# Row-wise largest absolute value: two-row loads into a column ring, a computed tail, and loads through GpSimd's queue

## The chip, the cores and the metric

The kernel runs on one core of a Trainium2 chip. The metric is the device time of one execution in microseconds. The time of before is the median of 10 runs.

## The reference

The input is a matrix of 8192 x 8192 float32 (268.4 MB). For each row the largest absolute value is wanted, 8192 numbers:

```python
def reference(x):
    return np.linalg.norm(x, ord=np.inf, axis=1)
```

## The kernel before

The rows are cut into 64 blocks of 128. In a block each row lies on its own partition, and its 8192 columns lie along the partition. For each block t the kernel takes one of five rotating buffers `xt` (128 x 8192, 32 KB a partition), loads the block by SP's queue (`nc.sync.dma_start`, L55) and reduces it on VectorE (L59: `tensor_reduce` with max and absolute value). The result is one column of `res`, which is 128 x 64.

The first 54 blocks are loaded in one piece of 4 MB. The last ten follow the list `COOLDOWN`: seven blocks in two pieces of 4096 columns, one in 4096, 2048, 2048, one in four of 2048, one in 2048, 2048, 1536, 1280, 1280. A block in pieces leaves its maxima in `partial`, and a second reduction (L68) joins them into `res`. That makes 80 loads in all.

After the loop `make_identity` builds a unit matrix on GpSimd (its work is done in the first 1.3 us of the trace, since nothing stands before it there). TensorE transposes `res` into PSUM (L78), VectorE copies it to SBUF (L80), and one store of 64 rows of 128 numbers ends the kernel (L81).

The framework puts in all waits: a load into `xt` waits until the reduction of the block five back has read that buffer, and a reduction waits for its load. It also sets the order of each engine's queue: it keeps the order of the program among what is ready, and takes what is ready sooner ahead of what still waits.

Of the kernel before, what the change touches and what calls it, by code (L numbers as in the profile page):

```python
# [1 line left out]

# [5 lines left out]


COOLDOWN = (
    [[4096, 4096]] * 7
    + [[4096, 2048, 2048]]
    + [[2048, 2048, 2048, 2048]]
    + [[2048, 2048, 1536, 1280, 1280]]
)


@with_exitstack
def kernel(  # L20
    ctx: ExitStack,
    tc: tile.TileContext,
    x: bass.AP,
    out: bass.AP,
):
    nc = tc.nc
    P = 128
    n_rows, n_cols = x.shape
    assert n_rows % P == 0

    T = n_rows // P
    if n_cols == 8192 and T >= len(COOLDOWN):
        chunks = [[n_cols]] * (T - len(COOLDOWN)) + COOLDOWN
    else:
        chunks = [[n_cols]] * T

    x_t = x.rearrange("(t p) m -> t p m", p=P)

    pool = ctx.enter_context(tc.tile_pool(name="sbuf", bufs=5))
    single = ctx.enter_context(tc.tile_pool(name="single", bufs=1))  # L40
    psum_pool = ctx.enter_context(tc.tile_pool(name="psum", bufs=1, space=bass.MemoryType.PSUM))

    res = single.tile([P, T], mybir.dt.float32)
    maxch = max(len(c) for c in chunks)
    if maxch > 1:
        partial = single.tile([P, maxch], mybir.dt.float32)

    for t in range(T):
        ch = chunks[t]
        assert sum(ch) == n_cols  # L50
        xt = pool.tile([P, n_cols], x.dtype)
        off = 0
        for h, w in enumerate(ch):
            dst = res[:, t : t + 1] if len(ch) == 1 else partial[:, h : h + 1]
            nc.sync.dma_start(  # L55
                out=xt[:, off : off + w],
                in_=x_t[t, :, off : off + w],
            )
            nc.vector.tensor_reduce(  # L59
                out=dst,  # L60
                in_=xt[:, off : off + w],
                axis=mybir.AxisListType.X,
                op=mybir.AluOpType.max,
                apply_absolute_value=True,
            )
            off += w
        if len(ch) > 1:
            nc.vector.tensor_reduce(  # L68
                out=res[:, t : t + 1],
                in_=partial[:, : len(ch)],  # L70
                axis=mybir.AxisListType.X,
                op=mybir.AluOpType.max,
            )

    ident = single.tile([P, P], mybir.dt.float32)
    make_identity(nc, ident)
    res_t_psum = psum_pool.tile([T, P], mybir.dt.float32)
    nc.tensor.transpose(res_t_psum, res, ident)  # L78
    res_t = single.tile([T, P], mybir.dt.float32)
    nc.vector.tensor_copy(out=res_t, in_=res_t_psum)  # L80
    nc.sync.dma_start(out=out.rearrange("(t p) -> t p", p=P), in_=res_t)  # L81


# [1 line left out]
_INS = ['x']  # L85
_OUTS = [((8192,), 'float32')]


# [23 lines left out]
```

## Time and profile before

| what | us |
|---|---|
| median of 10 runs | 634.68 (634.54 to 634.91) |
| profiled execution, its own time | 634.92 |
| its span in the profile | 633.1 |
| VectorE busy | 559.0 (91 instructions) |
| POOL (GpSimd) busy | 0.7 (6 instructions) |
| loads issued | 80, all by SP's queue |
| a 4 MB load, issue to landing, median | 39.8 |
| the store, issue to landing | 1.8 |

The span runs from the first instruction of the program to the last thing that the profile records; the execution's own time has some 1.8 us around it. "SPq" is SP's queue, which only issues transfers here. Idle time of an engine is given with what ended it ("<-DMA xt<-in_x_dram" is a load into `xt`). DMA slices are fortieths of the span, 15.83 us each.

### The profile page before, as it was taken

To read this page: it belongs to the slowest core of one execution; us is meant where nothing else is said; L and a number is where in the kernel's file an instruction comes from. 1 tells how busy PE (TensorE), PEld (TensorE's weight loads), DVE (VectorE), ACT (ScalarE), POOL (GpSimd) and SP (SyncE) were. 2 spreads that over 40 slices of the span, in tenths; PEclk is the share of its full clock that TensorE was granted. 3 is DMA by queue.
4 is the path that set the end of the run, shared out by engine and by line. 5 is a ranking of instruction groups with operands and counts; after the bars stand their busy time and mean duration, and the time that the engine had idled before them with its cause. 6 is when DMAs were issued, how large, how long until landed. Compare 5 with 4: busy or idle time off the path is not lost.

```text
span 633.1 us, 294 instructions
## 1 busy us (share of the span) xinstructions
PE 0.4 (0%) x1; PEld 0.1 (0%) x1; DVE 559.0 (88%) x91; POOL 0.7 (0%) x6
## 2 busy tenths in 40 slices
PE   0000000000000000000000000000000000000000
PEld 0000000000000000000000000000000000000000
DVE  1988988988989889889898898898988989999997
POOL 0000000000000000000000000000000000000000
DMA  9999999999999999999999999999999999999995
GB/s 373 435 439 435 435 431 433 433 431 431 431 431 431 431 431 431 431 431 431 431 431 435 433 429 431 431 435 435 437 433 437 431 431 417 426 430 424 428 422 212
DMA packets 11602, 268.49 MB, mean 424 GB/s; under 512 B 1296, under 2 KB 1360, under 8 KB 1744
## 3 DMA queue, kind: packets, MB, share of 16 engines
q1 hardware_dynamic: 11600, 268.47, 98.9%
q14 instruction: 2, 0.02, 0.0%
HBM read 268.44 MB, written 0.03 MB: 424 GB/s over the span
## 4 chain that ended last, share of the span: by engine, by line
DMA 75%; DVE 24%; SPq 0%; issue 0%; PE 0%; DVEq 0%
DMA xt<-in_x_dram 75%; DVE res L59 15%; DVE partial L59 8%; SPq L55 0%; DVE res L68 0%; PE res_t_psum L78 0%; DVE res_t L80 0%; DVEq L59 0%
## 5 line engine op out<-in xcount | busy, mean ns | idle before, releaser
L59 DVE TENSOR_REDUCE res<-xt 128x1 f32<-128x8192 f32 x54 | 469.0, 8686 | 67.6 <-DMA xt<-in_x_dram 67.6
L59 DVE TENSOR_REDUCE partial<-xt 128x1 f32<-128x4096 f32 (+3 forms) x26 | 88.2, 3430 | 3.0 <-DMA xt<-in_x_dram 2.8
L68 DVE TENSOR_REDUCE res<-partial 128x1 f32<-128x2 f32 (+3 forms) x10 | 1.6, 156 | 0.3
L80 DVE COPY res_t<-res_t_psum 64x128 f32<-64x128 f32 x1 | 0.3, 282 | 0.6 <-PE res_t_psum L78 0.6
L78 PE MATMUL res_t_psum<-ident,res 128*64 128x128 f32 x1 | 0.4, 393 | 629.7 <-DVE res L68 629.7
masks.py:199 POOL TENSOR_SCALAR_AFFINE_SELECT ident<-ident 128x128 f32<-128x128 f32 x1 | 0.3, 292 | 0.1
L78 PEld LDWEIGHTS res_t_psum<-ident,res 128*64 128x64 f32 x1 | 0.1, 128 | 629.7 <-issue 629.7
masks.py:197 POOL MEMSET ident<- 128x128 f32 x1 | 0.2, 204 | 0.3 <-POOLq L96 0.3
L96 POOL MEMSET const-bfloat16-1.0<- 128x1 bf16 x1 | 0.1, 102 | 0.0
L96 POOL MEMSET const-uint8-127<- 128x1 uint8 x1 | 0.1, 102 | 0.0
L96 POOL MEMSET const-float32-0.0<- 128x1 f32 x1 | 0.1, 98 | 0.2 <-issue 0.2
L96 POOL MEMSET const-float32-1.0<- 128x1 f32 x1 | 0.1, 98 | 0.0
## 6 DMA issues: line engine op xcount, KB each, us to landing
xt<-in_x_dram SPq DMA_DIRECT2D x54, 4096.0 KB, 39.8
xt<-in_x_dram SPq DMA_DIRECT2D x15, 2048.0 KB, 39.0
xt<-in_x_dram SPq DMA_DIRECT2D x8, 1024.0 KB, 28.3
xt<-in_x_dram SPq DMA_DIRECT2D x2, 640.0 KB, 17.9
xt<-in_x_dram SPq DMA_DIRECT2D x1, 768.0 KB, 19.3
out_dram<-res_t SPq DMA_DIRECT2D x1, 32.0 KB, 1.8
```

Of the source, the lines that this page charges most:

```text
L59: nc.vector.tensor_reduce(out=dst, in_=xt[:, off : off + w], axis=mybir.AxisListType.X, op=mybir.AluOpType.max, apply_absolute_value=True,)
L68: nc.vector.tensor_reduce(out=res[:, t : t + 1], in_=partial[:, : len(ch)], axis=mybir.AxisListType.X, op=mybir.AluOpType.max,)
L78: nc.tensor.transpose(res_t_psum, res, ident)
L80: nc.vector.tensor_copy(out=res_t, in_=res_t_psum)
L96: nc = _bacc.Bacc("TRN2", target_bir_lowering=False, num_devices=1)
```

## The change

The diff replaces the five buffers by one ring of 3 x 16384 columns (192 KB a partition) with 16 columns of padding behind it, and works as follows.

- **Large loads.** Two neighbouring rows go to one partition, so that a load takes 128 runs of 64 KB, 8 MB in all. One reduction makes both maxima (`res_big[:, t, :]`). There are `n_big` such loads, and the ring holds three.
- **Tail.** `tail_pieces` works the last blocks out backwards from a last piece of 1088 columns. It has a cost for a load and one for a reduction (`LOAD`, `REDUCE`: us a column, us each), and makes each earlier piece as large as the time lets it. With these constants it gives 14 blocks of 128 rows in 28 pieces: seven of 8192 columns, four of 4096 + 4096, then 2432, 2432, 3328, then 1728, 1728, 2496, 2240, and last 1408, 1472, 1600, 1408, 1216, 1088. So `n_big` is 25, and there are 53 loads.
- **Waits written by hand.** Each load counts on one of eight semaphores of the kernel's own, and its reduction waits on that. A load also waits for the reduction eight loads back. Where a load overwrites what a reduction reads, the framework still puts in the wait.
- **Joining.** The maxima of a tail block in pieces are joined by `tensor_scalar` with max on GpSimd (nine in all), in the place of L68. The last block's partial maxima are put into the columns just behind its last piece, so that its last reduction takes them along.
- **Output.** TensorE transposes the maxima of the large blocks and of the tail blocks but the last, ScalarE copies them, and SP stores them (two stores, `store_early`). The last block's 128 maxima are transposed in 32 x 32 squares on VectorE and stored as four lines of 32.
- **Queue.** All loads are issued by GpSimd (`self.nc.gpsimd.dma_start`), which makes their descriptors in software, in the place of SP's hardware queue. `make_identity` stands ahead of them in the program, on the same engine.

The diff, cut to its core:

```diff
+R = 2
+RING = 3 * 16384
+PAD = 16
+SEMS = 8
+LOAD = (1.1775e-3, 0.075)
+REDUCE = (1.0417e-3, 0.060)
+FIRST = 1088
+GRAIN = 64
+
+def tail_pieces(n_cols, big):
+    slack = 0.0
+    lag = REDUCE[0] * FIRST + REDUCE[1]
+    rows = []
+    while True:
+        left, row = n_cols, []
+        while left:
+            w = FIRST if not rows and not row else int((lag + slack - REDUCE[1]) / REDUCE[0])
+            w = max(GRAIN, w // GRAIN * GRAIN)
+            if w >= left:
+                w = left
+            elif 2 * w > left:
+                w = (left // 2 + GRAIN - 1) // GRAIN * GRAIN
+            row.append(w)
+            left -= w
+            slack += (LOAD[0] - REDUCE[0]) * w + LOAD[1] - REDUCE[1]
+        rows.append(row[::-1])
+        if (lag + slack - REDUCE[1]) / REDUCE[0] > big:
+            return rows[::-1]
...
+    def load(self, at, w, src):
+        i = self.started
+        self.started += 1
+        ins = self.nc.gpsimd.dma_start(out=self.ring[:, at : at + w], in_=src)
+        ins.then_inc(self.sems[i % SEMS], 16)
...
+        if i >= SEMS:
...
+            self.tc.add_manual_dep(
+                ins.ins,
+                self.reductions[i - SEMS].name,
...
+    def reduce(self, dst, src):
+        i = len(self.reductions)
+        ins = self.nc.vector.tensor_reduce(
...
+        ins.wait_op(self.sems[i % SEMS], 16 * (i // SEMS + 1), "sem-ge")
...
-    for t in range(T):
-        ch = chunks[t]
...
-            nc.sync.dma_start(
-                out=xt[:, off : off + w],
-                in_=x_t[t, :, off : off + w],
-            )
...
+    make_identity(nc, ident)
+    pieces = Pieces(tc, ring)
+
+    for t in range(n_big):
+        at = pieces.room(R * n_cols)
+        pieces.load(at, R * n_cols, x_big[t])
+        buf = ring[:, at : at + R * n_cols]
+        pieces.reduce(res_big[:, t, :], buf.rearrange("p (r m) -> p r m", r=R))
...
+    for t, widths in enumerate(tail):
...
+        for w, at in zip(widths, spots):
+            pieces.load(at, w, x_tail[t, :, col : col + w])
+            col += w
+        for i, (w, at) in enumerate(zip(widths, spots)):
+            behind = n - 1 if final and i == n - 1 else 0
+            pieces.reduce(parts[i], ring[:, at : at + w + behind])
+        if n > 1 and not final:
+            best = parts[0]
+            for i in range(1, n):
+                dst = res_tail[:, t : t + 1] if i == n - 1 else parts_t[:, n + i - 1 : n + i]
+                nc.gpsimd.tensor_scalar(
+                    out=dst, in0=best, scalar1=parts[i], scalar2=None, op0=mybir.AluOpType.max
+                )
+                best = dst
+    store_early()
+
+    turn = nc.vector.transpose(out=last_t, in_=last)
+    pieces.after_loads(turn)
+    tc.declare_fence(turn.ins, group="loads")
+    nc.sync.dma_start(
+        out=out_tail[n_tail - 1].rearrange("(b k) -> b k", k=32),
+        in_=last_t.rearrange("(b c) k -> c b k", c=32)[0],
+    )
```

## Prediction

> **What bounds the kernel now.** I read the page first: engine shares, then the two rows of slices, then the costliest groups.
>
> ```profile
> span 633.1 us, 294 instructions
> PE 0.4 (0%) x1; PEld 0.1 (0%) x1; DVE 559.0 (88%) x91; POOL 0.7 (0%) x6
> DMA  9999999999999999999999999999999999999995
> GB/s 373 435 439 435 435 431 433 433 431 431 431 431 431 431 431 431 431 431 431 431 431 435 433 429 431 431 435 435 437 433 437 431 431 417 426 430 424 428 422 212
> L59 DVE TENSOR_REDUCE res<-xt 128x1 f32<-128x8192 f32 x54 | 469.0, 8686 | 67.6 <-DMA xt<-in_x_dram 67.6
> ```
>
> VectorE is 88% busy, but its idle time ends on a load: 67.6 us before the 54 big reductions. The DMA engines are full in every slice but the last; only the first (373 GB/s), the tail (417 to 430) and the last (212) stand below 431. So the loads set the time, and three places are left: the start, what a load costs beside its bytes, and what follows the last landing. The timeline gives all three.
>
> ```profile
> 12.96 8.69 DVE L59 TENSOR_REDUCE res<-xt 128x1 f32<-128x8192 f32 x1 [12.96 <-DMA xt<-in_x_dram]
> 22.67 8.69 DVE L59 TENSOR_REDUCE res<-xt 128x1 f32<-128x8192 f32 x1 [1.02 <-DMA xt<-in_x_dram]
> ...
> 527.93 8.69 DVE L59 TENSOR_REDUCE res<-xt 128x1 f32<-128x8192 f32 x1 [1.02 <-DMA xt<-in_x_dram]
> ...
> 577.82 4.42 DVE L59 TENSOR_REDUCE partial<-xt 128x1 f32<-128x4096 f32 x1 [0.40 <-DMA xt<-in_x_dram]
> ...
> 587.61 4.42 DVE L59 TENSOR_REDUCE partial<-xt 128x1 f32<-128x4096 f32 x1 [0.41 <-DMA xt<-in_x_dram]
> ```
>
> Each reduction here starts when its load lands. 53 steps from 12.96 to 527.93 give 9.716 us for a 4 MB row block in one load. A block in two loads takes 587.61 - 577.82 = 9.79. The second load costs 0.074 us, and the bytes (9.716 - 0.074) / 8192 = 1.177 ns a column. The first landing, 12.96, less one step leaves 3.24 us that are spent once: some 2.15 before data flow at full rate (the first slice moved 5.90 MB in 15.83 us, at the later 431.7 GB/s 13.68 us of work), some 1.1 from a load's last bytes to the reduction. All 524,288 columns in 80 loads: 617.1 + 5.9 = 623.0; plus 3.24, the last landing is at 626.2. The end is then
>
> ```profile
> 620.49 8.92 DVE L59 TENSOR_REDUCE partial<-xt 128x1 f32<-128x2048 f32 x5
> 629.44 0.16 DVE L68 TENSOR_REDUCE res<-partial 128x1 f32<-128x5 f32 x1
> 629.75 0.39 PE L78 MATMUL res_t_psum<-ident,res 128*64 128x128 f32 x1 [629.75 <-DVE res L68]
> 630.18 0.28 DVE L80 COPY res_t<-res_t_psum 64x128 f32<-64x128 f32 x1 [0.58 <-PE res_t_psum L78]
> 630.49 0.55 SPq L81 DMA_DIRECT2D out_dram<-res_t  x1
> ```
>
> VectorE is about 3.2 us behind when the data are in; then a combining reduction, TensorE, a copy, and 2.6 us of store. That is 6.9 us after the last landing.
>
> **What the Trainium skill says.** "DMA: Bandwidth & Descriptors" (Latency and other measured facts) puts the first byte of a software-generated load at about 1 us, of a hardware one at 0.6; before has only the second kind. The same page (Issuing engines are not separate DMA queues) says that all issuers end on the same 16 engines; no run here shows loads from GpSimd. Its Bandwidth section fits software loads as 2.0 us plus bytes / 436e3, nearly the 435 GB/s that 1.177 ns a column means, but lists 425 GB/s as the best it measured: I use these as the two ends. "SBUF — State Buffer" (Who interferes with whom) says that a reduction on VectorE never takes the ports it shares with GpSimd, so descriptor writing is not held up by it. Nothing before tests that, as POOL is done at 1.3 us.
>
> **The change, part by part.** The sizes that the diff works out are 25 loads of 16384 columns (8 MB), then 14 tail blocks of 28 pieces (the title says 31): seven of 8192, four of 4096+4096, then 2432, 2432, 3328; 1728, 1728, 2496, 2240; 1408, 1472, 1600, 1408, 1216, 1088.
>
> Fewer loads: 53 instead of 80 at 0.074 is -2.0 us, if a 64 KB run moves as fast per byte as a 32 KB one. Not shown before; I take the same, within 0.2% (1.2 us) either way.
>
> Start: POOL's queue has the constants and the identity first, and these end at 1.01 + 0.29 = 1.30 us, while SP issued its first load at 0.74. That is +0.56, and the skill's first-byte difference adds 0.4: +0.96. From below +0.56; from above I allow +4, as POOL may prepare its queue.
>
> Steady stretch: load i waits for the reduction three back, since the ring holds three. A big reduction takes 16384 x 1.042 ns + 0.15 = 17.2 us (slope and constant from the 8192 and 4096 rows, 8686 and 4417 ns), a load 19.36, so load i is issued some 21 us before its turn. One or two microseconds of descriptor making are hidden by that: zero. If the cover went, each of some 50 loads would show them.
>
> Tail: the wait for the reduction eight back leaves 11 us or more in the queue even at the last load, worked out from the same steps. Zero. On VectorE, a back-to-back reduction costs its columns x 1.042 ns + 0.063 (two of 4096 in 8.75 us). Stepping through the 28 pieces it starts 7.4 us behind after the last 8 MB piece, falls to 0.2 at the last piece, and never idles long enough to matter. The ten combining reductions of L68 (1.6 us) leave VectorE. In their place nine tiny maxima come to POOL's queue, between loads; each waits for a tail block's last reduction, and what is queued behind it is a later load. POOL's 128x1 memset takes 0.1 us; I take 0.2 for each maximum. The scheduler places what is ready sooner ahead, so I expect in front of a maximum only loads whose own wait ends earlier: zero; the other order is a rival.
>
> Early stores: three TensorE transposes, three ScalarE copies, two SP stores, all before the last block is in; 32 KB beside 268 MB is under 0.1 us, hidden by some 10 us of final-block loads.
>
> End: final reduction 1093 x 1.042 + 0.148 = 1.29; backlog 0.2; gaps 0.05; VectorE transpose of 32 columns 0.18 (the 5-column reduction takes 0.16; between 0.15 and 0.4); store and finish 2.61 as now. Sum 4.3 instead of 6.9.
>
> **Sum.** Last landing 3.24 + 0.96 + 617.1 + 3.9 = 625.2; plus 4.3 the span is 629.5 against 633.1: 2.0 from loads, 2.6 from the end, less 0.96. The profiled execution took 634.92, 1.8 more than its span, and the median is 634.68, 0.24 less. So 631.3 profiled, 631.1 as median; I put 0.4 on top for POOL's part of the start: 631.5.
>
> **Rivals.** Software loads are slower each or per byte. At 425 GB/s a column is 1.205 ns: +14.4 us, 645.5. At 0.2 us a load instead of 0.074, 53 x 0.126 = 6.7: 637.8. It decides from small numbers: 4.5 us spends the gain and 0.2% more, that is 0.085 us a load or 0.73% of rate. For it: the skill's 425, and that hardware generation already runs within 0.1% of the fit's ceiling, so a change can only lose. Against: each engine gets eight long runs for 19 us, little to generate or fetch. This is the main case on the slower side.
>
> The maxima block the loads. If POOL keeps the written order, after each of six tail blocks the next block's loads stand behind a maximum that waits for the block's last reduction. The DMA engines then run dry for 1.1 (landing) + 4.4 (reduction) + 0.1 + 0.2 (maximum) + about 2 (new load) = 7.8 us, thrice; 11.7 at the first, where VectorE is behind, 7.2 and 6.3 at the two with shorter pieces: 48.6 us in all, some 680.
>
> A costly start: POOL needs 3 to 6 us before its first load. All of it lies on the path: 633.5 to 637.
>
> The late start and the new end cancel, and loads gain nothing (64 KB runs slower by 0.3%): 633.5, no change.
>
> **How the numbers follow.** A difference of 0.2% (1.3 us) is about what a measurement of this kernel can tell from no change. My forecast, between 630 and 633.4, gets 0.48; no change (633.4 to 635.9), from a start of 2 to 4 us more or a rate 0.4% lower, 0.12; slower loads 0.25; a start beyond 5 us 0.05; blocked loads or a much worse rate 0.10. That is 0.48 faster, 0.12 same, 0.40 slower. The range runs from 629.3 (64 KB runs 0.2% quicker, start +0.56) to 646 (425 GB/s), leaving out the blocked case and what is worse. Since both signs count, the likeliest case's own range is 629.3 to 633.4.
>
> **What would show it.** Right: the first big reduction near 23.6 us (19.36 + 4.2), later ones 19.36 apart, slices at 431 to 435 GB/s from the second on, the queue's kind software, the last reduction 1.3 us long and ending near 626.7, 2.8 us before the end. Steps above 19.5 would show the slower loads; gaps in the slices after 560 us with POOL's maxima ahead of loads, the blocked queue; a first landing beyond 26 us, the start. A step of 19.45 or more, or a drained slice in the tail, makes the forecast wrong.

## The result, and the profile after

The changed kernel takes 645.19 us (median of 8 runs, 644.82 to 646.81), the kernel before 634.68. The ratio is 1.0167 with a 95% interval of 1.0158 to 1.0176: slower by 1.7%, where 631.5 us was forecast. The profiled execution took 645.17 us with a span of 643.0.

The page of the changed kernel, its span, engine shares and DMA slices (now 16.1 us each), its queue, and the big reductions:

```profile
span 643.0 us, 182 instructions
PE 1.0 (0%) x3; PEld 0.3 (0%) x3; DVE 552.9 (86%) x54; ACT 2.0 (0%) x4; POOL 31.3 (5%) x68
DMA  9999999999999999999999999999999999997896
GB/s 391 391 457 400 448 457 391 457 432 416 457 432 416 457 408 440 457 391 457 457 391 457 457 391 457 436 412 457 420 428 424 425 435 444 413 388 328 322 384 223
...
q0 software_dynamic: 7632, 268.44, 97.6%
...
L88 DVE TENSOR_REDUCE res_big<-ring 128x2 f32<-128x16384 f32 x25 | 430.5, 17220 | 75.4 <-DMA ring<-in_x_dram 75.4
```

For 34 of the 40 slices the loads run as before. The single slices are uneven now (391, 457), but their mean from the second on is 432 GB/s, as before. The loss is in the last slices: 413, 388, 328, 322, 384, where before had 417 to 430. The timeline of VectorE bounds it:

```profile
23.42 17.22 DVE L88 TENSOR_REDUCE res_big<-ring 128x2 f32<-128x16384 f32 x1 [23.42 <-DMA ring<-in_x_dram]
...
488.70 17.22 DVE L88 TENSOR_REDUCE res_big<-ring 128x2 f32<-128x16384 f32 x1 [2.14 <-DMA ring<-in_x_dram]
```

The first large load lands at 23.42 us (23.6 was forecast). The last lands at 488.70, which is (488.70 - 23.42) / 24 = 19.39 us a step, where 19.36 was forecast. Up to here the forecast is half a microsecond off. The rest is lost in the tail. There POOL's own timeline shows what its queue did (start, duration, instruction, idle time before it and what ended that):

```profile
532.00 1.05 POOL L72 DMA_DIRECT2D ring<-in_x_dram  x2 [7.55 <-DVE res_tail L88]
574.84 0.28 POOL L188 TENSOR_SCALAR res_tail<-parts 128x1 f32<-128x1 f32 x1 [41.79 <-DVE parts L88]
575.07 0.58 POOL L72 DMA_DIRECT2D ring<-in_x_dram  x1
583.49 0.27 POOL L188 TENSOR_SCALAR res_tail<-parts 128x1 f32<-128x1 f32 x1 [7.85 <-DVE parts L88]
583.72 1.10 POOL L72 DMA_DIRECT2D ring<-in_x_dram  x2
```

POOL issues a pair of loads at 532.00 ("x2") and then nothing for 41.79 us. It stands at the first joining maximum, which waits for a reduction on VectorE (`parts`). The next load comes the moment that the maximum is done, at 575.07, and the next again only behind the second maximum. The chain of work that ended last has the same steps (start, duration, what):

```profile
583.49 0.23 POOL res_tail L188
583.72 7.43 DMA ring<-in_x_dram
591.15 0.02 issue
591.17 4.43 DVE parts L88
595.60 0.09 issue
595.70 0.23 POOL res_tail L188
595.92 7.48 DMA ring<-in_x_dram
```

A maximum releases a load, the load lands 7.4 us later (4.8 us of bytes, the rest start and landing), the reduction takes 4.4 us, and only that releases the next maximum. So in the tail, loads and reductions take turns where they should run beside each other. The size follows from the rate at which the DMA engines moved data (the last number of each line, in GB/s). The first line is the changed kernel from 575 to 630 us. The second is the variant with all maxima last (below) in the same part of its tail, 575 to 620 us:

```profile
575.00:630.00 55.00, 0.39 (x1) 0.10 (x1) 45.01 (x14) 0.24 (x1) 9.82 (x23) 1.00 0.85 332
```

```profile
575.00:620.00 45.00, 0.39 (x1) 0.10 (x1) 45.00 (x15) 0.26 (x1) 8.20 (x21) 1.00 1.00 422
```

At 332 instead of 422 GB/s, 55 x (1 - 332 / 422) = 11.7 us are lost. VectorE's idle times in the tail, from the timeline, add up to 3.46 + 0.46 + 2.96 + 1.78 + 1.06 + 0.21 + 0.80 + 1.20 = 11.9 us. The two spans differ by 13.4 us. The rest of that: the tail begins 0.5 us later (505.84 against 505.32 us), and VectorE is busy 0.9 us longer (552.9 against 552.0).

### The profile page after: what moved, and what is told of

It is laid out like the page before. It is cut to its first block, busy times and chain, and to the rows that moved or that the text cites. A ratio compares the mean times of both kernels' runs of the same rounds, so it can differ in the third digit from the quotient of the medians.

```text
span 643.0 us, 182 instructions
## 1 busy us (share of the span) xinstructions
PE 1.0 (0%) x3; PEld 0.3 (0%) x3; DVE 552.9 (86%) x54; ACT 2.0 (0%) x4; POOL 31.3 (5%) x68
## 4 chain that ended last, share of the span: by engine, by line
DMA 59%; DVE 39%; issue 1%; POOL 0%; POOLq 0%; DVEq 0%
DMA ring<-in_x_dram 59%; DVE res_big L88 24%; DVE res_tail L88 9%; DVE parts L88 5%; DVE ring L88 1%; POOL res_tail L188 0%; DVE last_t L194 0%; POOL ident masks.py:197 0%; POOLq L188 0%; POOLq masks.py:199 0%; DVEq L88 0%; POOLq L213 0%
## 5 line engine op out<-in xcount | busy, mean ns | idle before, releaser
L88 DVE TENSOR_REDUCE res_big<-ring 128x2 f32<-128x16384 f32 x25 | 430.5, 17220 | 75.4 <-DMA ring<-in_x_dram 75.4
L88 DVE TENSOR_REDUCE parts<-ring 128x1 f32<-128x4096 f32 (+5 forms) x15 | 52.8, 3560 | 10.0 <-DMA ring<-in_x_dram 9.9
L88 DVE TENSOR_REDUCE res_tail<-ring 128x1 f32<-128x8192 f32 x7 | 60.2, 8675 | 0.0
L72 POOL DMA_DIRECT2D ring<-in_x_dram x53 | 28.5, 539 | 513.1 <-DVE res_big L88 489.2
L88 DVE TENSOR_REDUCE ring<-ring 128x1 f32<-128x1408 f32 (+4 forms) x6 | 9.3, 1573 | 2.1 <-DMA ring<-in_x_dram 2.0
L188 POOL TENSOR_SCALAR res_tail<-parts 128x1 f32<-128x1 f32 x6 | 1.6, 274 | 76.2 <-DVE parts L88 76.2
```

What stands on the lines that cost most here:

```text
L72: ins = self.nc.gpsimd.dma_start(out=self.ring[:, at : at + w], in_=src)
L88: ins = self.nc.vector.tensor_reduce(out=dst, in_=src, axis=mybir.AxisListType.X, op=mybir.AluOpType.max, apply_absolute_value=True,)
L188: nc.gpsimd.tensor_scalar(out=dst, in0=best, scalar1=parts[i], scalar2=None, op0=mybir.AluOpType.max)
```

## The experiments

**The maxima on VectorE.** The loads stay on GpSimd's queue.

```diff
-                nc.gpsimd.tensor_scalar(
+                nc.vector.tensor_scalar(
```

> The nine maxima go from GpSimd's queue to VectorE; all 53 loads stay on GpSimd's software queue. Blocked-queue theory: the eight idle stretches of VectorE in the tail of the changed kernel (3.46 + 0.46 + 2.96 + 1.78 + 1.06 + 0.21 + 0.80 + 1.20 = 11.9 us) go away, and nine maxima at about 0.16 us come to VectorE, whose backlog takes most of them: 631.8 to 634 us. Rival, software loads of a megabyte or less are slow in themselves: the idle stretches stay, since no load is changed, and the time is 643 to 647 us.

Measured: 633.68 us (633.38 to 633.92), 0.9983 of before (0.9976 to 0.9991). The idle stretches are gone: the waits table shows none of VectorE on loads in the tail. So loads of a megabyte or less are not slow in themselves. But VectorE is now busy without a break until the end, and each maximum takes 0.21 us there. The span (median 631.9) is 2.0 us longer than the next variant's (629.85), about nine times 0.21. The time is only 1.6 us longer, for a reason that the last section gives.

**The maxima behind the last load.** They stay on GpSimd, and only their place in the queue changes.

```diff
+            joins.append((t, n, parts, parts_t))
...
+    for t, n, parts, parts_t in joins:
...
+            ins = nc.gpsimd.tensor_scalar(
...
+            tc.add_manual_dep(
+                ins.ins,
+                pieces.last_load.name,
+                mybir.DependencyInfo(mybir.DependencyClass.NoSync, mybir.DependencyReason.DATA),
...
```

> The nine maxima stay on GpSimd, but all stand behind the last load in its queue. Blocked-queue theory: the loads are again limited only by the reduction eight back, VectorE does not wait in the tail, 631.5 to 633.5 us. Rival, that GpSimd computing at all slows its descriptor making or VectorE: the work is the same, so 640 us or more. Rival, slow small software loads: 643 to 647 us.

Measured: 632.05 us (631.82 to 632.29), 0.9957 of before (0.9942 to 0.9972), span 629.6. The instructions are the same (54 on VectorE, 68 on POOL, as in the changed kernel); the order in POOL's queue alone is worth 645.19 - 632.05 = 13.1 us. POOL's timeline of this variant, in the time in which the changed kernel's stood still:

```profile
531.48 1.05 POOL L72 DMA_DIRECT2D ring<-in_x_dram  x2 [7.54 <-DVE res_tail L89]
540.07 0.53 POOL L72 DMA_DIRECT2D ring<-in_x_dram  x1 [7.55 <-DVE res_tail L89]
548.67 0.53 POOL L72 DMA_DIRECT2D ring<-in_x_dram  x1 [8.07 <-DVE res_tail L89]
557.26 0.53 POOL L72 DMA_DIRECT2D ring<-in_x_dram  x1 [8.06 <-DVE res_tail L89]
565.85 0.53 POOL L72 DMA_DIRECT2D ring<-in_x_dram  x1 [8.06 <-DVE res_tail L89]
570.18 0.53 POOL L72 DMA_DIRECT2D ring<-in_x_dram  x1 [3.80 <-DVE parts L89]
```

Five loads were free to go between 540 and 570 us: their own waits ended there. In the changed kernel all five stood behind the first maximum.

**All loads on SP's hardware queue.**

```diff
-        ins = self.nc.gpsimd.dma_start(out=self.ring[:, at : at + w], in_=src)
+        ins = self.nc.sync.dma_start(out=self.ring[:, at : at + w], in_=src)
```

> The same kernel with its 53 loads on SP's hardware queue; the maxima stay on GpSimd. Every theory expects no blocked loads here. The prediction's sum without the 0.96 us of the later start is 630.1 to 630.6 us. If the software queue costs more than its start and its order, this is lower than the run with late maxima by more than 1.5 us; if the start is all, by 0.7 to 1.3 us.

Measured: 630.86 us (630.75 to 631.03), 0.9938 of before (0.9923 to 0.9953), span 628.6. This is the fastest of all versions, ahead of both kernels. The first landing is at 22.66 us instead of 23.81 with the maxima last, 1.15 earlier, and the whole is 1.2 us faster.

**The kernel before, with only its 80 loads on GpSimd's queue.**

```diff
-            nc.sync.dma_start(
+            nc.gpsimd.dma_start(
                 out=xt[:, off : off + w],
```

> The kernel before with only its 80 loads moved to GpSimd's queue; no other work stands between them there. Blocked-queue theory: only a later start, by 0.3 to 1 us, so 635 to 636 us. Rival, each software load costs some 0.2 us instead of 0.074: 80 x 0.126 = 10 us more, 645 us; rival, the rate is 425 GB/s: 649 us.

Measured: 635.55 us (635.31 to 635.94), 1.0014 of before (1.0007 to 1.0021), which is 0.9 us. Its first reduction starts at 14.05 us where before had 12.96. The 54th starts at 528.87 where before had 527.93, so the mean step is 9.71 us in both. So a software load costs the start, and while loads stand ready in the queue it costs nothing more per load or per byte than a hardware load.

**Five loads ahead.** The maxima stay between the loads, but each is put behind the load five after the piece that it waits for. In the changed kernel this was one to three.

```diff
+        while self.joins and self.joins[0][0] <= i:
+            self.join(*self.joins.pop(0)[1:])
...
+                pieces.joins.append((first + i + 5, dst, best, parts[i]))
```

> The nine maxima stay between the loads in GpSimd's queue, but each stands behind the load five after the piece that it waits for, where the changed kernel has one to three. Queue-order theory: five loads still in flight when the maximum is released are more than a new load needs to start, so nothing runs dry: 631.7 to 632.5 us, as with all maxima last. Rival, that any maximum between loads costs time (a switch of GpSimd between computing and descriptor making, on the path): nine times 0.3 us and more, 635 us or above.

Measured: 632.16 us (631.88 to 632.81), 0.9962 of before (0.9948 to 0.9976), as with all maxima last. A maximum between loads does no harm by itself. What counts is how much is still in flight when it is released.

**One maximum only.** The first keeps the place that it had; the other eight go behind the last load (the same edit, with 2 for the first maximum and the last load for the rest).

> Only the first maximum (tail block 7) keeps its place two loads ahead; the other eight stand behind the last load. Queue-order theory: one stretch without data of 1.8 to 2.3 us ahead of the third load after it, and the rest as with all maxima last: 633.5 to 634.6 us. If VectorE's backlog of some 4 us at that place hid the gap, 632.0 us; if one late load were enough to upset the whole tail, 640 us or more.

Measured: 633.53 us (633.22 to 634.41), 0.9983 of before (0.9976 to 0.9989). That is 1.5 us above the variant with all maxima last, a little below the 1.8 to 2.3 us that were expected for the gap. The loss is at the expected place, 285 GB/s from 575 to 580 us and 442 in the next five:

```profile
575.00:580.00 5.00, 0.00 (x0) 0.00 (x0) 5.00 (x2) 0.00 (x0) 3.83 (x8) 1.00 0.79 285
580.00:585.00 5.00, 0.00 (x0) 0.00 (x0) 5.00 (x2) 0.00 (x0) 0.66 (x2) 1.00 1.03 442
```

The maximum was released at 575.08 us, POOL issued the next load at 575.31, and cut into tenths of a microsecond the trace shows no data from 575.5 to 576.6 and less than the full rate until about 578. VectorE's backlog did not hide the gap, since it moves every later landing: VectorE works without a break until 592 us and then waits 0.40 + 0.47 + 0.26 + 0.27 = 1.4 us for loads.

**The first load on SP, the other 52 on GpSimd,** with the maxima last. The first load gets a semaphore of its own.

```diff
-        ins = self.nc.gpsimd.dma_start(out=self.ring[:, at : at + w], in_=src)
+        ins = (self.nc.gpsimd if i else self.nc.sync).dma_start(out=self.ring[:, at : at + w], in_=src)
```

> The maxima behind the last load, and the first of the 53 loads issued by SP, the other 52 by GpSimd. Start theory: what is left between late maxima on the software queue (632.05) and all loads on SP (630.86) is the start alone, so 630.8 to 631.2 us. If each software load costs a little more, 631.6 to 632.1 us.

Measured: 631.43 us (631.13 to 631.53), 0.9947 of before (0.9933 to 0.9962). It lies between the two expectations, and half of the 1.2 us came back. So the start is part of what remains, and the other half isn't settled by this run, because it brought a new effect: the first landing came late, with SP's load and the next one on GpSimd's queue in flight at once. VectorE's first line in the timeline, in a view that ends at 130 us:

```profile
39.57 102.85 DVE L90 TENSOR_REDUCE res_big<-ring 128x2 f32<-128x16384 f32 x6 [39.57 <-DMA ring<-in_x_dram]
```

**The program's order, strictly.** Each tail block's loads stand behind the last maximum of the block before.

```diff
+        if self.behind is not None:
+            self.tc.add_manual_dep(
+                ins.ins,
+                self.behind.name,
+                mybir.DependencyInfo(mybir.DependencyClass.NoSync, mybir.DependencyReason.DATA),
...
+                pieces.behind = ins.ins
```

> The prediction's rival in full: each tail block's loads stand behind the maximum of the block before (the order in which the program is written). The prediction priced that at 48.6 us more than an unblocked queue, six stretches without data: 632.05 + 48.6 = 680.6 us; with a new load starting in 1.8 to 2.3 us, 679 to 682 us. If blocked loads cost less than that sum (landing 1.1 + reduction 4.4 + maximum + new load), 660 us or less.

Measured: 678.68 us (678.48 to 678.88, two runs), 1.0693 of before. The span is 676.7, 47.1 us above that of the variant with all maxima last; 48.6 were priced. One stall in its timeline:

```profile
587.44 4.42 DVE L96 TENSOR_REDUCE parts<-ring 128x1 f32<-128x4096 f32 x1 [0.47 <-DMA ring<-in_x_dram]
591.96 0.27 POOL L196 TENSOR_SCALAR res_tail<-parts 128x1 f32<-128x1 f32 x1 [15.94 <-DVE parts L96]
592.19 1.10 POOL L73 DMA_DIRECT2D ring<-in_x_dram  x2
599.82 4.42 DVE L96 TENSOR_REDUCE parts<-ring 128x1 f32<-128x4096 f32 x1 [7.96 <-DMA ring<-in_x_dram]
```

From the issue at 592.19 to the landing at 599.82 are 7.63 us. Less 4.82 for the bytes (4096 x 1.177 ns) and the prediction's 1.1 for the landing, a new load into an empty queue needs some 1.7 us to start; the prediction took 2.

## Why the prediction was wrong, by its own steps

**The step that failed** is the sentence on the tail: the scheduler places what is ready sooner ahead, so in front of a maximum stand only loads whose own wait ends earlier, and the cost is zero. The queue is fixed when the kernel is built. The order in it left five loads that could have gone between 540 and 570 us behind a maximum that waited until 574.84. The prediction argued from the rule of the scheduler, as if it knew the chip's times, and so put the blocked queue into a rival with little chance. The rival had its mechanism and place right, and weak slices after 560 us, the sign that was named for it, are what the page shows. But it was drawn as all or nothing: 48.6 us for the strict order. The real order lay between, with one to three loads ahead of a maximum, and cost 13.1 us instead of zero.

One rule fits all the orders that were run: a gap opens where the bytes still in flight at a maximum's release take less time than the maximum and a new load's start. In the variant with one maximum 0.4 us of bytes were left (575.08 to 575.5), and the next load needed 0.23 until its issue and some 1.7 to start: a gap of 1.5 us, as measured. With nothing in flight the full stall of the strict order follows, and with five loads ahead there is no gap. The limit between was not tried. Nor was it tried why the scheduler's plan put the maxima there; only what the order does was.

**A chance agreement.** The measured 645.19 us lies beside the 645.5 that the prediction gave for software loads at 425 GB/s, and so inside its wide range. That rival is refuted by the steps below; the agreement of the numbers is chance.

**The rest of the sum held,** as the variant with all maxima last shows, which is the kernel that the prediction had in mind: a span of 629.5 was worked out and 629.6 measured. As a time, 631.5 us was forecast and 632.05 measured, and this closeness is partly luck. The 0.4 us that were put on top for POOL's part of the start are there, but they lie outside the span, and with all loads on SP's queue they are there as well (last section).

- Fewer loads: steps of 19.35 us in that variant from its second load on (43.12, 62.48, 81.84), 19.36 forecast. So a 64 KB run moves as fast per byte as a 32 KB one, with the same 0.074 us for each load.
- Start: 0.96 was forecast. GpSimd's first landing came 0.8 to 1.15 us after SP's (23.42 to 23.81 in six kernels, against 22.66). Of this 0.55 is the later issue, 1.26 to 1.28 instead of 0.72. The forecast had 0.56 for it, but not for the right reason: the kernel before with its loads on GpSimd has no identity ahead of them and also issues its first at 1.26. What holds the first issue until then stays open. From the issue on, the trace shows the first data after 1.02 us on SP's queue and after 1.36 to 1.40 on GpSimd's. The difference of 0.36 agrees with the 0.4 between the two figures that the Trainium skill gives in "DMA: Bandwidth & Descriptors", Latency and other measured facts.
- Rate: the rival of slower software loads is refuted. 8.39 MB in 19.35 us is 433.5 GB/s, above the 425 that the same page lists in its section Bandwidth as the best it measured. (The fit with 436e3, the prediction's other end, stands on that page under Anatomy of one DMA, not under Bandwidth, and the 435.0 GB/s of 1.177 ns a column lie 0.2% below it, not 0.1%.)
- Ports: the 25 big reductions took 17.219 to 17.221 us each beside software loads, and 17.22 with hardware loads. This agrees with "SBUF — State Buffer", Who interferes with whom: a reduction on VectorE isn't held up by GpSimd.
- End: 4.3 us were forecast after the last landing. With all maxima last the final reduction began at 625.58 us, where 625.2 and a backlog of 0.2 were forecast. The parts measured after that are 1.30 for the final reduction, 0.21 for the transpose (0.18 forecast), 0.03 from there to the store's issue, and 2.45 to the end of the span.
- A maximum on GpSimd: 0.27 us, 0.2 assumed. With five loads ahead of each this cost the span nothing.

So the change is two changes. The ring, the large loads and the new end bring 634.67 - 630.86 = 3.8 us; the software queue takes 14.3 us back, of which 13.1 are order and 1.2 what is left of the queue itself. Loads on SP's queue keep the gain.

## What to carry to other kernels

A queue that issues loads should hold nothing that waits for the results of those loads. Where it must, count for each such instruction what is still in flight when it is released: as long as that lasts longer than the instruction and a new load's start (2 us here), the rule above says that it costs nothing. Below that the gap went to the end in full here, where the loads set the time. If loads are moved to another engine, read that engine's queue in the order in which it was built, not the order in which things could run.

## What the runs showed that was not expected

- Two queues with 8 MB loads in flight share the engines, as the time of the landing tells. The first load landed at 39.57 us where it lands at 22.66 with all loads on the one hardware queue. VectorE then ran eight reductions without a break, until it had caught up. The time at the end was not hurt, as the loads set it.
- A software load holds POOL for 0.53 us whatever its size here (0.5 to 8 MB); the first of all took 0.66 to 0.72, and one right after a maximum 0.58.
- A tail that is planned to leave VectorE 0.2 us at the last piece has no room for 1.6 us of small work. The same nine maxima cost the span nothing that can be seen on GpSimd behind the loads, and their full time on VectorE.
- The maxima on GpSimd do cost something outside the span. A run's time is 1.7 to 1.8 us above its span in the kernel before, also with its loads on GpSimd, and with the maxima on VectorE. It is 2.1 to 2.25 us above it in every variant that has the maxima on GpSimd, whichever queue issues the loads. The changed kernel and the first variant differ in nothing else, so these 0.4 us belong to the maxima; what they are spent on the runs don't show.
